# Withdrawing the 64-byte start alignment of the activation and weight part buffers in a two-layer decoder trunk

## The chip, the core and the metric

The kernel runs on one core of a Trainium2 chip. The metric is the device time of one execution in microseconds (us), taken as the median of several runs. The profile is that of one execution. Its span is the time from the first to the last instruction of the core. TensorE is the matrix engine (PE in the profile, its weight loads are PEld), VectorE is DVE, ScalarE is ACT, GpSimd is POOL, and SyncE, which issues most DMAs, is SP.

## What is computed

The reference is a decoder trunk of two layers on 256 positions with 2048 features, in float32. Layer 0 has a recurrent mixer, layer 1 a dilated attention with 16 heads, and each is followed by a squared-ReLU MLP with 8192 hidden features.

```
def squared_relu_mlp(h, w1, w2):
    return jnp.square(jax.nn.relu(h @ w1)) @ w2

def reference(x, ...):
    h = x
    for layer in range(DEPTH):                       # DEPTH = 2
        hn = rms_norm(h, norm_mix[layer])
        if layer % 2 == 0:
            mix = recurrent_mixers(hn, ...)          # w_in, gates, conv, two recurrences, w_out
        else:
            mix = dilated_attention(hn, positions, w_qkv, w_o)
        h = h + mix
        h = h + squared_relu_mlp(rms_norm(h, norm_mlp[layer]), mlp_w1[layer], mlp_w2[layer])
    return rms_norm(h, final_norm)
```

## The kernel before

**Parts.** The matrix products run in TensorE's `float32r` type. To keep float32 accuracy each operand is split into two parts: a rounded one and the remainder. `hi = round(w)` is made by ScalarE (line 104) and `lo = w - hi` by VectorE (line 105). The product of two such numbers is summed from three matmuls, high by high, high by low and low by high. Every matmul goes through the helper `mm`, whose line is 176, so nearly all matmuls of the profile stand under L176.

**Weights.** A weight unit is 128 partitions by 2048 float32, that is 8192 bytes in each partition, fetched by one DMA of SP into one of three `raw` buffers. The class `Weights` (lines 93 to 109) takes one of three `hi` and one of three `lo` buffers for it and splits it. Units are fetched in a fixed order, two ahead of use (`unit`, `fetch`).

**Activations.** `bufa` holds the normalised input of the running layer, `bufb` the output of the mixer or the hidden features of the MLP. Both have for each of 16 blocks of 128 features 256 high and 256 low values, that is 32768 bytes in each partition. `split_to` (lines 228 to 235) writes them.

**Which operand streams.** In `project` (functions `cross` and `direct`) a 128x128 block of `hi` or `lo` is loaded as weights, and `bufa` (in the gates `bufb`) is streamed, 512 or 256 columns at a time. In `tokens` and `products` it is the other way round: a 128x128 block of `bufa`, `bufb` or `forms` is loaded, and 512 columns of `hi` or `lo` are streamed. `forms` holds split sums of activations for a product by seven instead of eight block products in the second matrix of the MLP; it lives in a pool of its own (`pair0`, `pair1`), which exists only during an MLP. A `products` call works in groups of 12 matmuls (four blocks, three part products), each group with `bufb` alone or `forms` alone.

**Order.** The order of the matmuls is written out by hand: every `mm` gets an order dependency on the one before. The other engines are ordered by a planner, from priorities (`stream`, `urgent`) and its own clock. Pools of SBUF tiles are stacked one behind the other in the order of the code: `cst`, `act`, `wraw`, `whi`, `wlo`, `tmp`, and then the pools of each stage, which are closed and reused.

**Where the buffers lie.** This is the memory map of the built kernel before, in bytes from the start of a partition. Every tile's size is rounded up to 32 bytes (the 2056 bytes of `tab_` take 2080). A pool that holds a tile with `align_bytes=64` reserves 32 bytes more for each such tile, and the tile's start is rounded up to 64 within it.

| tile | start | size | start modulo 64 | start modulo 128 |
|---|---|---|---|---|
| first tile of `cst` | 16512 | | 0 | 0 |
| `xall` (first of `act`) | 20800 | 16384 | 0 | 64 |
| `bufa` | 37184 | 32768 | 0 | 64 |
| `bufb` | 70016 | 32768 | 0 | 0 |
| `raw`, first of three | 102784 | 8192 | 0 | 0 |
| `hi`, first of three | 127360 | 8192 | 0 | 0 |
| `lo`, first of three | 152000 | 8192 | 0 | 64 |
| `t1` (first of `tmp`) | 176576 | 1024 | 0 | 64 |
| stage pools, from | 183200 | | 32 | 32 |
| `hz`, first, attention | 195488 | 1024 | 32 | 32 |
| `forms`, layer 0 | 187328 | 16384 | 0 | 64 |
| `forms`, layer 1 | 191424 | 16384 | 0 | 64 |
| `zp`, first, layer 0 | 203712 | 1024 | 0 | 64 |
| `a`, layer 0 | 208832 | 8192 | 0 | 64 |

`bufa` ends at 69952, `bufb` starts 64 bytes later. The last `hi` buffer ends at 151936, the first `lo` buffer starts 64 bytes later. The pool ahead of `forms` in layer 0 ends at 187296, and `forms` starts 32 bytes later; in layer 1 it ends at 191392.

Of the kernel before, what the change touches and what calls it, by code (L numbers as in the profile page):

```python
# [11 lines left out]
F32R = mybir.dt.float32r  # L12
# [7 lines left out]
P = 128  # L20
S = 256
D = 2048
KB = D // P
# [17 lines left out]
def trunk_kernel(ctx, tc, x, xtok, cols, tab, masks, pos, fin, w_in, w_gate, w_out, w_qkv, w_o, w1, w2, out):  # L41
# [3 lines left out]
    act = pool("act")  # L45
    wraw = pool("wraw", 3)
    whi = pool("whi", 3)
    wlo = pool("wlo", 3)
# [9 lines left out]
    xall = act.tile([P, KB * S], F32, name="xall")  # L58
    xin = xall.rearrange("p (k s) -> p k s", s=S)
    xres = xall.rearrange("p (j d) -> p j d", j=2)  # L60
    bufa = act.tile([P, KB, 2 * S], F32R, name="bufa", align_bytes=LINE)
    bufb = act.tile([P, KB, 2 * S], F32R, name="bufb", align_bytes=LINE)

    units = []
    made = {}
# [27 lines left out]
    class Weights:  # L93
        def __init__(self, raw, step=2048):
            self.raw = raw
            self.hi = whi.tile([P, 2048], F32R, name="hi", align_bytes=LINE)
            self.lo = wlo.tile([P, 2048], F32R, name="lo", align_bytes=LINE)
            for at in range(0, 2048, step) if step else ():
                self.split(at, step)

# [754 lines left out]
LINE = 64  # L855
# [108 lines left out]
```

## Time and profile before

| | |
|---|---|
| time, median of 3 runs | 2227.1 us (2226.89 to 2227.21) |
| the profiled execution's own time | 2227.31 us |
| its span | 2225.5 us |
| granted TensorE clock, mean | 0.998 |
| PE busy | 2207.2 us (99%), 12004 matmuls |
| PEld busy | 1892.6 us (85%) |
| DVE busy | 1673.0 us (75%) |
| ACT busy | 1110.0 us (50%) |
| DMA | 431.25 MB, mean 194 GB/s |

The busy times of PE count the overlap of successive matmuls once, and the end of a matmul is modelled; what a stream of matmuls really costs is seen best from where the next one starts, that is from the chain of work that ended last, whose pieces have a start, a length and a count. In the groups of instructions, `p<-hi,bufb` reads: output `p`, inputs `hi` and `bufb`, with the line, the number of instructions after an x, the busy time in all and the mean of one in ns, and then the idle time of the engine ahead of them and what ended it.

### The profile page before, as it was taken

How to read it: one execution, taken by the hardware profiler on the slowest of the kernel's cores; microseconds unless marked ns; L12 is line 12 of the kernel's file. 1: busy time of each engine (PE TensorE's matmuls, PEld its weight loads, DVE VectorE, ACT ScalarE, POOL GpSimd, SP SyncE). 2: the span in 40 equal slices, each digit the busy share in tenths (PEclk: the TensorE clock that was granted, in tenths of full speed). 3: DMA queues.
4: the chain of work that ended last, by engine and by line, in shares of the span. 5: the costliest groups of instructions: out<-in, count | busy, mean ns of one | idle time of the engine just before them, and what ended most of it. 6: DMA issues, size and time to landing. Idle time of an engine off the chain costs nothing.

```text
span 2225.5 us, 29702 instructions
## 1 busy us (share of the span) xinstructions
PE 2207.2 (99%) x12004; PEld 1892.6 (85%) x12004; DVE 1673.0 (75%) x2286; ACT 1110.0 (50%) x1364; POOL 15.8 (1%) x23
## 2 busy tenths in 40 slices
PE   9999999999999999999999999999999999999997
PEld 8999998888888888888888888888878888888886
DVE  8777796578777877877867878556787687687787
ACT  6444585444445444544654444444454454454454
POOL 0000000000000000000000000000000000000000
PEclk9999999999999999999999999999999999999999
DMA  8444446556655755755654544655566567566553
GB/s 312 163 158 163 158 154 228 180 185 203 229 187 186 242 196 174 244 199 159 208 207 158 182 173 164 224 179 185 158 218 241 171 201 247 188 189 246 190 189 114
DMA packets 61017, 431.25 MB, mean 194 GB/s; under 512 B 6784, under 2 KB 7552, under 8 KB 9424
## 3 DMA queue, kind: packets, MB, share of 16 engines
q1 hardware_dynamic: 58320, 412.20, 52.8%
q0 software_dynamic: 2560, 17.16, 4.2%
q8 instruction: 94, 1.54, 0.3%
q14 instruction: 43, 0.35, 0.0%
HBM read 427.48 MB, written 2.10 MB: 193 GB/s over the span
## 4 chain that ended last, share of the span: by engine, by line
PE 95%; DVE 3%; ACT 1%; DMA 0%; issue 0%; SPq 0%; ACTq 0%; DVEq 0%
PE p L176 81%; PE po L176 6%; PE pd L176 5%; DVE lo L105 1%; PE pl L471 1%; ACT hi L104 1%; PE pl L179 0%; DVE a L142 0%; PE pl L777 0%; PE po L798 0%; DMA xall<-in_x 0%; PE pd L790 0%; DMA a<-in_w 0%; DVE bufa L234 0%; PE pd L455 0%
## 5 line engine op out<-in xcount | busy, mean ns | idle before, releaser
L105 DVE TENSOR_TENSOR lo<-raw,hi 128x1024 fp32r<-128x1024 f32 (+2 forms) x486 | 822.1, 1709 | 359.3 <-ACT hi L104 339.2
L104 ACT CAST hi<-raw 128x1024 fp32r<-128x1024 f32 (+2 forms) x486 | 688.3, 1441 | 685.2 <-PE p L176 524.9
L176 PE MATMUL p<-bufa,hi 128*128 128x512 f32 (+1 forms) x3840 | 862.8, 359 | 2.4 <-DVE bufa L234 2.3
L176 PEld LDWEIGHTS p<-bufa,hi 128*128 128x128 f32 x3840 | 668.1, 188 | 104.8 <-DVE bufa L234 3.8
L176 PE MATMUL p<-bufa,lo 128*128 128x256 f32 x3200 | 517.6, 283 | 0.0
L176 PEld LDWEIGHTS p<-bufa,lo 128*128 128x128 f32 x3200 | 449.4, 188 | 14.2
L176 PE MATMUL p<-hi,bufb 128*128 128x512 f32 x1408 | 458.0, 395 | 0.2 <-DVE xall L650 0.2
L176 PEld LDWEIGHTS p<-hi,bufb 128*128 128x128 f32 x1408 | 264.4, 188 | 64.1 <-DVE xall L650 3.1
L176 PE MATMUL p<-lo,bufb 128*128 128x512 f32 x704 | 277.8, 395 | 0.3 <-DVE lo L105 0.2
L104 ACT CAST hi<-a 128x2048 fp32r<-128x2048 f32 x64 | 122.0, 1906 | 160.9 <-PE p L176 83.6
L105 DVE TENSOR_TENSOR lo<-a,hi 128x2048 fp32r<-128x2048 f32 x64 | 146.5, 2289 | 55.5 <-ACT hi L104 55.4
L176 PEld LDWEIGHTS p<-lo,bufb 128*128 128x128 f32 x704 | 132.1, 188 | 33.1 <-DVE lo L105 2.7
L176 PE MATMUL p<-hi,bufa 128*128 128x512 f32 x384 | 125.1, 400 | 0.4 <-ACT hi L104 0.4
L176 PEld LDWEIGHTS p<-hi,bufa 128*128 128x128 f32 x384 | 72.3, 188 | 16.7 <-ACT hi L104 1.3
L176 PE MATMUL pd<-hi,bufb 128*128 128x512 f32 x256 | 85.5, 395 | 0.1
L176 PE MATMUL po<-hi,bufb 128*128 128x512 f32 x256 | 85.4, 394 | 0.1
L176 PE MATMUL p<-hi,forms 128*128 128x512 f32 x256 | 85.4, 394 | 0.0
L176 PE MATMUL p<-lo,bufa 128*128 128x512 f32 x192 | 76.5, 399 | 1.8 <-DVE lo L105 1.8
L142 DVE TENSOR_TENSOR a<-a,raw 128x2048 f32<-128x2048 f32 x32 | 73.0, 2282 | 0.0
L223 ACT COPY t<-p 128x256 f32<-128x256 f32 x128 | 47.0, 367 | 41.4 <-PE p L176 41.1
L650 DVE SCALAR_TENSOR_TENSOR xall<-p,nm,xall 128x512 f32<-128x512 f32 x64 | 47.7, 746 | 24.7 <-PE p L176 24.7
L230 ACT CAST bufb<-zp 128x256 fp32r<-128x256 f32 x128 | 50.8, 404 | 17.2 <-DVE zp L684 17.1
(239 smaller groups left out, 1807.9 us busy)
## 6 DMA issues: line engine op xcount, KB each, us to landing
raw<-in_w SPq DMA_DIRECT2D x224, 1024.0 KB, 4.8
raw<-in_w_qkv SPq DMA_DIRECT2D x48, 1024.0 KB, 4.8
raw<-in_w_in SPq DMA_DIRECT2D x46, 1024.0 KB, 4.8
raw<-in_w_out SPq DMA_DIRECT2D x16, 1024.0 KB, 4.8
a<-in_w SPq DMA_DIRECT2D x16, 1024.0 KB, 4.8
t<-in_w SPq DMA_DIRECT2D x16, 1024.0 KB, 4.9
t<-in_w POOLq DMA_DIRECT2D x16, 1024.0 KB, 8.0
raw<-in_w_o SPq DMA_DIRECT2D x16, 1024.0 KB, 4.9
```

Of the source, the lines that this page charges most:

```text
L104: A.copy(h, w)
L105: V.tensor_tensor(l, w, h.bitcast(F32), OP.subtract)
L142: V.tensor_tensor(r, r, held[add], OP.add)
L176: chain[:] = [after(T.matmul(*args, **kw), chain)]
L223: A.copy(t, p[:, S:])
L230: A.copy(dst[:, :S], src)
L471: T.matmul(pl[:, j], kq[:, js], halves(qp[:, js], c, True), start=True, stop=True)
L650: V.scalar_tensor_tensor(xres[:, j, at], bank, (r2 if sign > 0 else r2n)[:, j:j + 1], xres[:, j, at], op0=OP.mult, op1=OP.add)
```

## The change

The four tiles `bufa`, `bufb`, `hi` and `lo` are asked for without a start alignment. Nothing else of the program is edited: every instruction, its shape, its order dependency and its priority stand as before. `forms`, the buffer of the activation sums, keeps its alignment of 64 bytes in both layers (`LINE = 64`).

```
-    bufa = act.tile([P, KB, 2 * S], F32R, name="bufa", align_bytes=LINE)
-    bufb = act.tile([P, KB, 2 * S], F32R, name="bufb", align_bytes=LINE)
+    bufa = act.tile([P, KB, 2 * S], F32R, name="bufa")
+    bufb = act.tile([P, KB, 2 * S], F32R, name="bufb")
...
     class Weights:
         def __init__(self, raw, step=2048):
             self.raw = raw
-            self.hi = whi.tile([P, 2048], F32R, name="hi", align_bytes=LINE)
-            self.lo = wlo.tile([P, 2048], F32R, name="lo", align_bytes=LINE)
+            self.hi = whi.tile([P, 2048], F32R, name="hi")
+            self.lo = wlo.tile([P, 2048], F32R, name="lo")
```

## The prediction

> **What bounds the kernel now.** I read the page first: span, busy shares and the chain that ended last.
>
> ```profile
> span 2225.5 us, 29702 instructions
> PE 2207.2 (99%) x12004; PEld 1892.6 (85%) x12004; DVE 1673.0 (75%) x2286; ACT 1110.0 (50%) x1364; POOL 15.8 (1%) x23
> PE 95%; DVE 3%; ACT 1%; DMA 0%; issue 0%; SPq 0%; ACTq 0%; DVEq 0%
> PE p L176 81%; PE po L176 6%; PE pd L176 5%; DVE lo L105 1%; PE pl L471 1%; ACT hi L104 1%; PE pl L179 0%; DVE a L142 0%; PE pl L777 0%; PE po L798 0%; DMA xall<-in_x 0%; PE pd L790 0%; DMA a<-in_w 0%; DVE bufa L234 0%; PE pd L455 0%
> ```
>
> The kernel is a stream of matmuls: 92% of the span is L176 on the chain that sets the end. The splitting of the weights (L104, L105) is on it with 2%. So a change of where buffers lie is worth something only through the pace of the L176 matmuls, or if splitting or DMA became so slow that PE waits. Next I read the groups, shapes kept apart, for the pace of each operand pair; these rows carry all that follows.
>
> ```profile
> L176 PEld LDWEIGHTS p<-bufa,hi 128*128 128x128 f32 x3840 | 668.1, 188 | 104.8 <-DVE bufa L234 3.8 <-DVE hz L411 0.3
> L105 DVE TENSOR_TENSOR lo<-raw,hi 128x2048 fp32r<-128x2048 f32 x224 | 512.7, 2290 | 221.8 <-ACT hi L104 218.6 <-ACT bufb L230 3.2
> L176 PE MATMUL p<-hi,bufb 128*128 128x512 f32 x1408 | 458.0, 395 | 0.2 <-DVE xall L650 0.2
> L104 ACT CAST hi<-raw 128x2048 fp32r<-128x2048 f32 x224 | 428.1, 1911 | 463.2 <-PE p L176 377.9 <-PE po L176 54.5 <-PE pd L176 16.1
> L176 PE MATMUL p<-lo,bufb 128*128 128x512 f32 x704 | 277.8, 395 | 0.3 <-DVE lo L105 0.2
> L176 PEld LDWEIGHTS p<-hi,bufb 128*128 128x128 f32 x1408 | 264.4, 188 | 64.1 <-DVE xall L650 3.1
> L105 DVE TENSOR_TENSOR lo<-a,hi 128x2048 fp32r<-128x2048 f32 x64 | 146.5, 2289 | 55.5 <-ACT hi L104 55.4
> L176 PE MATMUL p<-hi,bufa 128*128 128x512 f32 x384 | 125.1, 400 | 0.4 <-ACT hi L104 0.4
> L104 ACT CAST hi<-a 128x2048 fp32r<-128x2048 f32 x64 | 122.0, 1906 | 160.9 <-PE p L176 83.6 <-DVE a L142 47.1 <-PE pd L176 18.9
> L176 PEld LDWEIGHTS p<-hi,bufa 128*128 128x128 f32 x384 | 72.3, 188 | 16.7 <-ACT hi L104 1.3
> L176 PE MATMUL p<-lo,bufa 128*128 128x512 f32 x192 | 76.5, 399 | 1.8 <-DVE lo L105 1.8
> L176 PE MATMUL p<-lo,forms 128*128 128x512 f32 x128 | 51.0, 399 | 0.0
> ```
>
> The reader is to see that a 512-column matmul takes 394 to 400 ns whichever buffer is streamed and loaded, that every weight load takes 188 ns, and that ScalarE and VectorE split a unit in about 1.91 and 2.29 us wherever it comes from.
>
> **The change part by part.** First, what it does to the addresses, since no instruction changes. I worked this out from the sizes in the code and the map of the kernel before. `bufa` starts where it did, at 37184: the tile ahead of it ends on a multiple of 64, so the request never moved it. Without the 32 reserved bytes of each of the two aligned tiles of `act`, `bufb` starts right at the end of `bufa`, 37184 + 32768 = 69952 = 1093 x 64. The `raw` buffers follow at 69952 + 32768 = 102720 = 1605 x 64, `hi` at 102720 + 3 x 8192 = 127296 = 1989 x 64, `lo` at 151872 = 2373 x 64, `tmp` at 176448 = 2757 x 64. So all of them are still multiples of 64: the sizes are, and the stack reaches them at one. Everything from `tmp` on moves down by 128 bytes and keeps its remainder, `forms` too (187200 and 191296, by its own request). What moves in the low bits is this: `bufb`, `raw` and `hi` go from a multiple of 128 to 64 beyond one; `bufa`, `lo`, `forms` stay 64 beyond one.
>
> Then the costs, each by a pair of rows that differs in that bit already. Streaming `hi` (and `lo`, past weights from `bufb`, `forms` or `bufa`, in `products` and `tokens`): before, `hi` starts at a multiple of 128 and `lo` does not, and `p<-hi,bufb` and `p<-lo,bufb` take 395 and 395 ns. Cost 0. Loading `hi` as weights: it becomes what `lo` is; the loads of `bufa` and of `bufb`, one on each side of that bit, take 188 and 188 ns, as the loads of `hi` itself do, and PEld sits idle for 104.8 us ahead of those. Cost 0.
>
> Loading `bufb`: it becomes what `bufa` and `forms` are, and here the means do differ a little, 395 against 400 and 399 ns. Ends of matmuls are modelled, so I looked at starts: first the chain of waits through `w_out` (96 matmuls with `bufb`) and through `products` (12 at a time; in this order with `bufb`, `forms`, `forms`, `bufb`), then the timeline of PE through a value projection of layer 1, which loads `bufa`.
>
> ```profile
> 362.95 22.28 PE p L176 x96
> ...
> 518.44 2.79 PE pd L176 x12
> ...
> 529.79 2.81 PE pd L176 x12
> ...
> 540.97 2.81 PE pd L176 x12
> ...
> 546.56 2.78 PE pd L176 x12
> ```
>
> ```profile
> 1139.19 0.63 PE L176 MATMUL p<-hi,bufa 128*128 128x512 f32 x2
> 1139.66 0.39 PE L176 MATMUL p<-lo,bufa 128*128 128x512 f32 x1
> ...
> 1146.13 0.63 PE L176 MATMUL p<-hi,bufa 128*128 128x512 f32 x2
> ```
>
> With `bufb`, 12 matmuls take 22.28 / 8 = 2.785 us or 2.78 to 2.79. With `bufa`, ten times three matmuls take 1146.13 - 1139.19 = 6.94 us, so 12 take 2.776. With `forms` they take 2.81. The start of `bufa` has the bit and is not slower, so the bit is not what makes `forms` slower; `forms` differs in more, for its high and low parts are 2048 bytes apart and those of `bufb` 1024. I take 0. The end above is that `bufb` comes to the price of `forms`: 2880 matmuls (1408 + 704 in `p`, 384 each in `pd` and `po`, rows below) are 240 groups at 2.81 - 2.785 = 0.025 us, +6.0 us. The end below is that the 768 matmuls with `forms` (16 calls of `products`, four groups of 12 in each), whose distance to `hi` changes by 64 bytes, come to 2.785: 64 groups, -1.6 us.
>
> ```profile
> L176 PE MATMUL pd<-hi,bufb 128*128 128x512 f32 x256 | 85.5, 395 | 0.1
> L176 PE MATMUL po<-hi,bufb 128*128 128x512 f32 x256 | 85.4, 394 | 0.1
> L176 PE MATMUL pd<-lo,bufb 128*128 128x512 f32 x128 | 50.4, 394 | 0.0
> L176 PE MATMUL po<-lo,bufb 128*128 128x512 f32 x128 | 50.4, 394 | 0.0
> ```
>
> Splitting: after the change `raw`, `hi` and `lo` start at the same remainder to 8192, as `raw` and `hi` do before. The tile `a` stands at another one, and `hi<-a` against `hi<-raw` is 1906 to 1911 ns, `lo<-a,hi` against `lo<-raw,hi` 2289 to 2290. No row has `lo` and `raw` at one remainder; at most I allow the 5 ns by which the ScalarE rows differ, 288 times 1.4 us, on two engines with 25% and 50% of idle time. On the path: 0.
>
> DMA into `raw`: it lands 64 bytes beyond a multiple of 128 after the change, which is where `a` lands before.
>
> ```profile
> raw<-in_w SPq DMA_DIRECT2D x224, 1024.0 KB, 4.8
> a<-in_w SPq DMA_DIRECT2D x16, 1024.0 KB, 4.8
> q1 hardware_dynamic: 58320, 412.20, 52.8%
> ```
>
> Both take 4.8 us, and a fetch is two units ahead. The cover, if it were slower, is the other half of the DMA engines' time. Cost 0.
>
> The order of instructions has no term: the planner goes by priorities and by which buffers are free, and tiles that share memory share it as before, since all the stage pools move by the same 128 bytes.
>
> The sum is 0. The profiled execution took 2227.31 us, 1.8 us more than its span, and 0.2 us more than the median of 2227.1; so the forecast is 2227.1 us. About 0.2%, 4.5 us, is what a measurement of this kernel can tell from no change.
>
> One thing I can't see is a `float32r` operand that starts off 64 bytes, because there is none before. The nearest rows are plain float32 matmuls: `hz`, at 32 beyond a multiple of 64, and `tab_` and `xall`, on multiples.
>
> ```profile
> L179 PE MATMUL pl<-tab__179,xall 128*128 128x128 f32 x96 | 12.4, 272 | 0.0
> L776 PE MATMUL pl<-hz 128*128 128x128 f32 x32 | 6.1, 272 | 0.0
> L415 DVE TENSOR_TENSOR hz<-p,t 128x256 f32<-128x256 f32 x32 | 13.2, 411 | 0.0
> L225 DVE TENSOR_TENSOR zp<-p,t 128x256 f32<-128x256 f32 x128 | 53.5, 418 | 4.4 <-ACT t L223 4.4
> ```
>
> They are equal on PE, 272 and 272 ns, and VectorE writes the unaligned `hz` in 411 ns and the aligned `zp` in 418. By these a start off 64 bytes is free; but float32 streams slower for each column than `float32r`, so for the latter I keep an upper end. It is one 64-byte piece more to read for each streamed operand, an estimate: 16 of 512 columns of 22.28 / 96 = 0.232 us is 7.25 ns, times 2880 + 768 + (384 + 192 with `bufa`) = 4224 streams of `hi` and `lo` is +30.6 us. It is paid only if a start falls off 64, which the arithmetic above excludes. The Trainium skill, SBUF — State Buffer, section Specifications (TRN2), gives "16-byte" cachelines as what a read should stay in; by that rule every start at a step of 32 bytes begins on a line, and this end would be 0 and not 30.6 us. The rows of `hz` and `xall` agree as far as float32 shows it; no run here shows it for `float32r`.
>
> **The rivals.** First, slower: loading `bufb` from 64 beyond a multiple of 128 costs what loading `forms` does. For it speak the 399 ns and the 2.81 us of `forms`, against it the 2.776 us of `bufa`, which has the same bit. It would give 2227.1 + 6.0 = 2233.1 us, slower by 0.27%. It decides from 0.019 us a group, 4.5 / 240.
>
> Second, slower: the tiles are not where I put them, and `hi` or `lo` comes to 32 beyond a multiple of 64, and the streams pay for it: 2227.1 + 30.6 = 2257.7 us. For it speaks that `forms` did need its 32 bytes, so starts off 64 exist in this stack; against it that all the tiles ahead of `lo` have sizes that are multiples of 64 and that the map of before fits the rule to the byte in five places. If that happens at half the price it is slower still, from 1.1 ns a stream.
>
> Third, faster: `forms` gets the pace of `bufb` because its distance to `hi` changes. That gives 2227.1 - 1.6 = 2225.5 us, which is within 0.2%. To go past 0.2% the dense stream as a whole would have to quicken; 4.5 us over the 12004 matmuls of the page is 0.4 ns each. Against it: before, `hi` and `lo` stand at different distances to `bufb` in that bit, and are streamed in the same 395 ns.
>
> **How the numbers follow.** No change in the pace: 0.87. First rival 0.05, second 0.02, third 0.04, of which 0.01 past 0.2%; another order or an effect of the addresses that no row shows, of either sign and past 0.2%, 0.02. So faster 0.02, within 0.2% 0.90, slower 0.08. The forecast is 2227.1 us. The range takes in both ends of the cost of loading: from 2225.5 to 2233.1 us.
>
> **What would show it.** Right: the same number of instructions on each engine; `p<-hi,bufb` and `p<-lo,bufb` within 1 ns of 395; groups of 12 with `bufb` at 2.78 to 2.79 us; weight loads at 188 ns; L104 and L105 at 1.91 and 2.29 us; DMA into `raw` at 4.8 us; idle time of PE as before. The first rival would show as groups of `bufb` at 2.81 us with the others unchanged, the second as longer streams of `hi` and `lo` in all of L176, the third as `forms` at 2.785 us. The prediction would be wrong by a cause I have not priced if L104 or L105 grew and PE's waits for them with it, or if the instructions stood in another order.

## The result and the profile after

The changed kernel takes 2206.7 us (median of 4 runs, 2206.14 to 2207.49) against 2227.14 us. The ratio is 0.9909 with a 95% interval of 0.9892 to 0.9926: 0.9% faster. The prediction was 2227.1 us, range 2225.5 to 2233.1: wrong.

Every engine runs the same instructions in the same order, and the memory map is the one worked out in the prediction (`bufb` 69952, `raw` 102720, `hi` 127296, `lo` 151872, `forms` 187200 and 191296). So addresses alone did this. First the page of the kernel after: span, busy times, the chain that ended last.

```profile
span 2204.3 us, 29702 instructions
PE 2180.6 (99%) x12004; PEld 1897.7 (86%) x12004; DVE 1673.1 (76%) x2286; ACT 1110.0 (50%) x1364; POOL 15.8 (1%) x23
PE 84%; DVE 9%; ACT 3%; DMA 2%; issue 1%; SPq 0%; ACTq 0%; DVEq 0%
```

PE is busy for 26.6 us less with the same 12004 matmuls. It is idle for 2204.3 - 2180.6 = 23.7 us, before 2225.5 - 2207.2 = 18.3, so 5.4 us of the gain went into waits. VectorE's share of the chain grew from 3% to 9%; that is the work through which the chain runs at those waits, not their length. Its busy time did not change. The groups, shapes kept apart, answer to those of the prediction:

```profile
L176 PE MATMUL p<-bufa,hi 128*128 128x512 f32 x2560 | 615.1, 392 | 2.4 <-DVE bufa L234 2.4
L176 PE MATMUL p<-bufa,lo 128*128 128x256 f32 x3200 | 521.9, 285 | 0.0
L105 DVE TENSOR_TENSOR lo<-raw,hi 128x2048 fp32r<-128x2048 f32 x224 | 512.7, 2290 | 209.5 <-ACT hi L104 206.3 <-ACT bufb L230 3.1
L176 PE MATMUL p<-hi,bufb 128*128 128x512 f32 x1408 | 451.9, 391 | 1.6 <-DVE xall L650 1.6
L104 ACT CAST hi<-raw 128x2048 fp32r<-128x2048 f32 x224 | 428.1, 1911 | 446.6 <-PE p L176 367.6 <-PE po L176 52.0 <-PE pd L176 13.0
L176 PE MATMUL p<-lo,bufb 128*128 128x512 f32 x704 | 275.3, 391 | 3.8 <-DVE lo L105 3.8
L176 PE MATMUL p<-hi,bufa 128*128 128x512 f32 x384 | 123.6, 396 | 0.7 <-ACT hi L104 0.7
L176 PE MATMUL p<-lo,forms 128*128 128x512 f32 x128 | 49.8, 389 | 0.0
```

Splitting is untouched (2290 and 1911 ns as before). All matmuls with 512 columns are shorter, 391 for 395 with `bufb` and, where `lo` is streamed past `forms`, 389 for 399. The row of 256 columns, `p<-bufa,lo`, takes 285 ns, 2 more than before. Here are the rows of before for the streams of `bufa`, which the prediction did not show, and from its chain the first product of an MLP quarter (16 units, 256 matmuls of 512 columns and 256 of 256):

```profile
L176 PE MATMUL p<-bufa,hi 128*128 128x512 f32 x2560 | 625.9, 396 | 2.3 <-DVE bufa L234 2.3
L176 PE MATMUL p<-bufa,lo 128*128 128x256 f32 x3200 | 517.6, 283 | 0.0
...
602.58 89.85 PE p L176 x512
```

The same place in the chain of the kernel after, with a matrix of `w_out` (96 matmuls with `bufb`) and groups of 12 in `products` (in this order with `forms`, `bufb`, `bufb`):

```profile
364.12 21.81 PE p L176 x96
...
581.23 2.72 PE po L176 x12
583.95 2.72 PE p L176 x12
586.67 2.72 PE po L176 x12
...
600.27 89.02 PE p L176 x512
```

The 96 take 21.81 us instead of 22.28, and groups of `forms` and of `bufb` cost the same now, 2.72 us instead of 2.81 and 2.78.

For the rest of this text the pace is worked out from the start times in the trace: the mean time from the start of one matmul to that of the next of its kind, leaving out those over 0.52 ns a column, which are waits. Which passages between groups are counted moves a mean by up to 0.2 ns. Before, the starts of a `products` group never settle (in a typical one 236, 237, 226, 235, 239, 234 ns with `forms`); after, they lie between 225 and 228. After the change a stream of `bufa` past `hi` needs some five matmuls of a unit to reach 227 ns, which makes its mean 228.4; before, it goes on alternating between 231 and 236. The gain by kinds of matmul:

| kind | count | before, ns | after, ns | us |
|---|---|---|---|---|
| `bufa` past `hi`, 512 columns | 2560 | 232.9 | 228.4 | -11.5 |
| `bufa` past `lo`, 256 columns, in `cross` | 2560 | 118.7 | 119.5 | +2.0 |
| `bufa` past both, 256 columns, in `direct` | 1920 | 118.2 | 119.7 | +2.9 |
| `hi`, `lo` past `bufb` | 2880 | 232.0 | 227.0 | -14.4 |
| `hi`, `lo` past `forms` | 768 | 234.0 | 226.7 | -5.6 |
| `hi`, `lo` past `bufa` | 576 | 231.6 | 228.4 | -1.8 |

That is -28.4 us; with 5.4 us more of idle PE it is -23.0, against -21.2 of the spans. Counted from start to start with every gap left in, the `L176` matmuls of 256 and 512 columns take 2124.1 us for 2145.0, which is 20.9 us less. So nearly all of the gain lies in them, and the waits and the passages from one kind to the next took back 7.5 us, more than the modelled ends of the matmuls show as idle time.

### The profile page after: what moved, and what is told of

The parts are those of the page before. It is cut to its first block, busy times and chain, and to the rows that moved or that the text cites. A ratio compares the mean times of both kernels' runs of the same rounds, so it can differ in the third digit from the quotient of the medians.

```text
span 2204.3 us, 29702 instructions
## 1 busy us (share of the span) xinstructions
PE 2180.6 (99%) x12004; PEld 1897.7 (86%) x12004; DVE 1673.1 (76%) x2286; ACT 1110.0 (50%) x1364; POOL 15.8 (1%) x23
## 3 DMA queue, kind: packets, MB, share of 16 engines
q0 software_dynamic: 2560, 17.16, 4.3%
## 4 chain that ended last, share of the span: by engine, by line
PE 84%; DVE 9%; ACT 3%; DMA 2%; issue 1%; SPq 0%; ACTq 0%; DVEq 0%
PE p L176 75%; DVE lo L105 5%; PE po L176 5%; DVE a L142 2%; ACT hi L104 2%; DMA a<-in_w 2%; PE pd L176 1%; PE pl L471 1%; DVE xall L650 1%; PE pl L179 0%; PE pl L777 0%; DVE bufa L234 0%; PE po L798 0%; DMA xall<-in_x 0%; PE pd L790 0%
## 5 line engine op out<-in xcount | busy, mean ns | idle before, releaser
L176 PE MATMUL p<-bufa,hi 128*128 128x512 f32 (+1 forms) x3840 | 854.5, 357 | 2.4 <-DVE bufa L234 2.4
L176 PEld LDWEIGHTS p<-bufa,hi 128*128 128x128 f32 x3840 | 672.0, 190 | 95.2 <-DVE bufa L234 3.8
L176 PE MATMUL p<-bufa,lo 128*128 128x256 f32 x3200 | 521.9, 285 | 0.0
L176 PEld LDWEIGHTS p<-bufa,lo 128*128 128x128 f32 x3200 | 452.6, 191 | 12.7
L176 PE MATMUL p<-hi,bufb 128*128 128x512 f32 x1408 | 451.9, 391 | 1.6 <-DVE xall L650 1.6
L176 PEld LDWEIGHTS p<-hi,bufb 128*128 128x128 f32 x1408 | 264.5, 188 | 59.1 <-DVE xall L650 5.0
L176 PE MATMUL p<-lo,bufb 128*128 128x512 f32 x704 | 275.3, 391 | 3.8 <-DVE lo L105 3.8
L176 PEld LDWEIGHTS p<-lo,bufb 128*128 128x128 f32 x704 | 132.3, 188 | 33.7 <-DVE lo L105 7.2
L176 PE MATMUL p<-hi,bufa 128*128 128x512 f32 x384 | 123.6, 396 | 0.7 <-ACT hi L104 0.7
L176 PEld LDWEIGHTS p<-hi,bufa 128*128 128x128 f32 x384 | 72.3, 188 | 16.0 <-ACT hi L104 1.6
L176 PE MATMUL pd<-hi,bufb 128*128 128x512 f32 x256 | 84.3, 390 | 0.2 <-DVE xall L650 0.2
L176 PE MATMUL po<-hi,bufb 128*128 128x512 f32 x256 | 84.2, 390 | 0.3 <-DVE xall L650 0.3
L176 PE MATMUL p<-hi,forms 128*128 128x512 f32 x256 | 84.1, 389 | 0.0
L176 PE MATMUL p<-lo,bufa 128*128 128x512 f32 x192 | 76.3, 397 | 1.8 <-DVE lo L105 1.8
```

The source lines that it names most:

```text
L176: chain[:] = [after(T.matmul(*args, **kw), chain)]
```

## The experiments

**The theories.** After the change `bufa`, `bufb`, `hi`, `lo` and `forms` all start at 64 modulo 256; before, they start at 64, 128, 128, 192 and 192. Theory D (distance): the pace of PE depends on how the start of the streamed buffer stands to that of the buffer whose blocks are loaded as weights. Theory S (place): a start 64 beyond a multiple of 128 is fast by itself. Theory W: reads of PE are disturbed by ScalarE and VectorE unless `raw`, `hi` and `lo` stand at one remainder. Blocks inside the buffers are multiples of 512 bytes apart, so the starts stand for all.

The buffers are moved by unused tiles between the pools; no instruction is added. For room in e2, e3 and e4, three small tiles of the last lines share the buffers of others, and `bufb` has a pool of its own, so that it can stand elsewhere in the stack.

```
     gap = lambda n, b: pool("gap_" + n).tile([P, b // 4], F32, name="gap_" + n)
...
     # e1: all together            gap("front", 64); act = pool("act")
     # e2: lo alone                gap("lo", 64); wlo = pool("wlo", 3); tmp = pool("tmp", 2); gap("stages", 128)
     # e3: hi alone, behind lo     gap("hi", 64); whi = pool("whi", 3)
     # e4: bufb alone, behind lo   gap("bufb", 64); actb = pool("actb")
```

Of the sixteen runs only e11, e12 and e13 were timed several times; each of the others is one execution.

**e1, all buffers 64 bytes further.**

> A gap of 64 bytes ahead of the buffers moves bufa, bufb, raw, hi, lo and forms together: their distances are those of the kernel after, but all of them now start at a multiple of 128. Theory D (distance: PE slows when the streamed buffer and the buffer loaded next stand at different remainders to 128 or 256): as the kernel after, 2206.7 us within 0.1%, starts of 512-column matmuls 227 ns apart in the steady stream. Theory S (place: a start 64 beyond a multiple of 128 is the fast one): as the kernel before or slower, 2227 us, 231 to 235 ns.

**e2, `lo` alone 64 bytes further.**

> From the kernel after, lo alone moves up by 64 bytes; hi, bufa, bufb and forms keep their places. Theory D: groups of 12 with bufb or forms, where lo is streamed between two streams of hi, lose their steady 227 ns and go back to about 231 to 235; the 512-column stream of bufa past hi keeps 227; the 256-column stream of bufa past lo goes from 119.5 back to about 118.7 ns. In all between 2210 and 2225 us. Theory S: lo at a multiple of 128 slows where lo is read only. Theory W (ScalarE and VectorE, reading raw and hi and writing lo, disturb PE's reads unless raw, hi and lo stand at one remainder): everything slows at once, the stream of bufa past hi too, 2227 us.

**e3, `hi` alone.**

> From the kernel after, hi alone moves by 64 bytes (its buffers now lie behind those of lo, so its upper address changes too). Theory D: the stream of bufa past hi goes back to about 233 ns for 512 columns, groups of 12 back to 231 to 235; about 2220 to 2230 us, the larger part of the 20 us lost. Theory S: the same sign, as hi is at a multiple of 128. Theory W: everything slows, 2227 us.

**e4, `bufb` alone.**

> From the kernel after, bufb alone moves by 64 bytes (it now lies behind lo). Theory D: groups of 12 with bufb slow to 231 to 235 ns a matmul, those with forms and the streams of bufa past hi and lo keep 227 and 119.5; 2880 matmuls by 5 ns less what VectorE's waits hide, 2212 to 2222 us. Theory S: the same place slows. Theory W: nothing slows, 2206.7 us, since raw, hi and lo keep their distances.

Measured: 2206.36, 2213.84, 2230.78 and 2219.71 us. From the chains, in the order e1, e2, e3, e4, a matrix of `w_out` (weights from `bufb`, streams of `hi` and `lo`) and a first product of the MLP (streams of `bufa`):

```profile
364.29 21.80 PE p L176 x96
...
600.50 89.02 PE p L176 x512
```

```profile
362.62 22.26 PE p L176 x96
...
600.93 88.64 PE p L176 x512
```

```profile
362.63 22.40 PE p L176 x96
...
602.82 90.05 PE p L176 x512
```

```profile
365.03 22.41 PE p L176 x96
...
604.08 89.05 PE p L176 x512
```

e1 keeps both lengths of the kernel after, although all starts are at multiples of 128 now: theory S falls. e4 leaves `raw`, `hi` and `lo` at one remainder and still slows the matmuls with `bufb` (233.3 ns), while the streams of `bufa` stay at 228.5 and those past `forms` at 228.0: theory W falls. e3, where `hi` is off all three of its partners, slows all kinds of 512 columns, to 233 ns, and ends 3.5 us above the kernel before. e2 shows what the prediction could not see: `hi` past `bufb` is at distance 0 there, and yet it runs at 232 ns, because in its groups of three `lo` at another distance stands between two streams of `hi`. One pair off its place takes the steady pace from the whole group. e2 also shows that 256-column streams like a distance: `bufa` past `lo` runs at 117.5 ns, and the first product of the MLP gets shorter, 88.64 for 89.02 us.

**Alignment itself, and the period.** The next four runs ask whether a start off 64 bytes costs anything, and at which distances PE is fast again. In three of them each kind of pair has a distance of its own, so that one run measures three.

```
     # e5: all, 32 bytes           gap("front", 32); ... ; gap("stages", 32); forms without align_bytes
     # e6: hi, lo +32, bufb +128, forms +160 against the kernel after
     # e7: bufb +96, hi, lo +128, forms 0
     # e8: bufb +128, hi, lo +256, forms +32
```

> A gap of 32 bytes ahead, and forms without its own request: all six buffers keep the distances of the kernel after, but every one starts 32 beyond a multiple of 64, which is what the alignment excluded. If only distances count: 2206.5 us within 0.1%, 227 ns. If a start off 64 bytes costs one more piece for each streamed operand, as my second rival had it: 4224 streams of 512 and 4576 of 256 columns by up to 7 ns, up to 2260 us.

> Measures three distances (streamed start minus loaded start) at once: bufa past hi and lo -32, hi and lo past bufb -96, hi and lo past forms -128. Theory D with a period of 128 bytes: forms runs at 227 ns, bufa and bufb wobble at 231 to 235. With a period of 256 or more: all three wobble. If what counts is a common line of 64 bytes, -32 would be half as bad as -64: about 230 ns. The 256-column streams past lo leave 119.5 for 117.5 to 118.7 where their distance is not 0. About 2222 to 2232 us if bufa and bufb are slow.

> Three more: bufa past hi and lo -128, hi and lo past bufb +32, hi and lo past forms +128. With a period of 128 bytes bufa runs at 227 and 119.5 ns and forms at 227, bufb at 231 to 235: about 2215 to 2220 us. With a period of 256 all wobble: 2225 to 2232 us.

> Tests the period from above: bufa past hi and lo -256, hi and lo past bufb -128, hi and lo past forms -32. With a period of 256 (or 128) bytes bufa runs at 227 and 119.5 ns; with a period of 512 it wobbles, 231 to 235. bufb as in the two runs ahead of it at 128, forms slow as at 32. 2212 to 2232 us.

Measured: 2206.24, 2233.03, 2231.79 and 2220.42 us. The same two rows of the chains of e5, e6, e7 and e8:

```profile
364.26 21.83 PE p L176 x96
...
600.62 89.02 PE p L176 x512
```

```profile
363.83 22.49 PE p L176 x96
...
604.38 89.92 PE p L176 x512
```

```profile
365.05 22.40 PE p L176 x96
...
605.01 89.87 PE p L176 x512
```

```profile
365.03 22.32 PE p L176 x96
...
603.99 89.03 PE p L176 x512
```

e5: starts 32 bytes beyond a multiple of 64 cost nothing, 2206.24 us with the lengths of the kernel after. The 64-byte alignment of these buffers was worth nothing as such. The Trainium skill, SBUF — State Buffer, section Specifications (TRN2), with its 16-byte lines agrees with this. e8 has `bufa` 256 bytes off `hi` and `lo` modulo 512 and is as fast there as at 0 (89.03 us), while 128 (e7 `bufa`, e8 `bufb`), 96 (e6 `bufb`) and 32 (e6 `bufa`, e7 `bufb`, e8 `forms`) are slow, 232 to 234 ns. So, on steps of 32 bytes, the period is 256 bytes, and nothing speaks for half the harm at 32: `bufa` past `hi` runs at 233.2 ns there.

**The change by halves.** From the kernel before, the alignment is withdrawn from two of the four tiles.

```
     # e9:  bufa and bufb without align_bytes; hi and lo as before
     # e10: hi and lo without align_bytes; bufa and bufb as before
```

> Half of the change: the alignment is withdrawn from bufa and bufb alone. By the map this puts bufa, bufb and hi at one remainder to 256 and lo and forms 64 beyond it. Theory D: bufa past hi keeps 227 to 228.5 ns, bufa past lo falls to about 117.5; every group of 12 matmuls in products and tokens has a stream at a distance (lo past bufb and bufa, hi past forms) and goes at 231 to 233. The same pattern as with lo alone moved, so 2213 to 2216 us. If the gain of the change belonged to single buffers and not to pairs, half of it or so would be here: 2217 us and no slow groups.

> The other half: the alignment is withdrawn from hi and lo alone. By the map bufb, hi, lo and forms come to one remainder to 256 and bufa 64 below it. Theory D: products and w_out, w_o at 227 ns; bufa past hi at 233 (2560 by 4.6 ns = +11.8 us against the kernel after), hi and lo past bufa at 232 (576 by 4 = +2.3), bufa past lo and the direct streams of 256 columns at about 117.6 (4480 by 1.9 = -8.5): 2206.7 + 5.6 = 2212 us.

e9 takes 2213.72 us, as expected: all groups with `hi` and `lo` streamed at 232 to 234 ns, `bufa` past `lo` at 117.6. e10 takes 2195.43 us, where 2212 was expected: faster than the whole change by 11 us. I timed it again, with an interval, and then varied the distance of `bufa` alone, with `hi`, `lo`, `bufb` and `forms` at one remainder.

> The kernel with the alignment withdrawn from hi and lo alone, timed with an interval. If one look was right: 2195 to 2196 us, ratio to the kernel before 0.985 to 0.988, 256-column streams past hi and lo at 113.8 ns again.

```
     # e14, e16: bufa in a pool of its own behind wlo, gap("bufa", 64) and gap("bufa", 32)
     # e15:      gap("bufb", 96) ahead of bufb, raw, hi, lo; forms along with them
```

> All at one remainder except bufa, which lies 64 bytes above (in the half change it lay 64 below). If only the size of the distance counts for the 256-column streams: 113.8 ns and 2195 us. If the sign counts: between 114 and 119.5 ns, 2195 to 2212 us. 512-column streams of bufa near 233 in both.

> All at one remainder except bufa, which lies 96 bytes below. If 113.8 ns at -64 is the bottom of a broad valley between 118.6 (-32) and 119.0 (-128): 114 to 117 ns, 2195 to 2206 us. If it is a single place: about 118.5 ns and 2214 to 2218 us.

> All at one remainder except bufa, which lies 32 bytes above. -32 gave 118.6 ns and 233.2. If the sign does not count the same: 2215 to 2220 us with products at 227. If it counts, anything between 113 and 119.5 ns.

Measured: e13 2196.07 us (4 runs, 2195.42 to 2196.34), ratio to the kernel before 0.9859, interval 0.9843 to 0.9875; e14 2199.03, e15 2216.81, e16 2209.93 us. First the groups of e13 that differ from the kernel after, then the two chain rows of e13, e14, e15 and e16:

```profile
L176 PE MATMUL p<-bufa,hi 128*128 128x512 f32 x2560 | 627.0, 396 | 2.4 <-DVE bufa L234 2.4
L176 PE MATMUL p<-bufa,lo 128*128 128x256 f32 x3200 | 503.5, 278 | 0.0
L176 PE MATMUL p<-bufa,hi 128*128 128x256 f32 x1280 | 229.1, 280 | 0.1
```

```profile
355.37 21.79 PE p L176 x96
...
591.39 88.76 PE p L176 x512
```

```profile
361.84 21.81 PE p L176 x96
...
597.29 88.27 PE p L176 x512
```

```profile
361.73 21.80 PE p L176 x96
...
599.20 90.22 PE p L176 x512
```

```profile
360.25 21.81 PE p L176 x96
...
597.12 89.56 PE p L176 x512
```

All four keep the fast 96 matmuls of `w_out`, 21.79 to 21.81 us. What differs is the stream of `bufa`, by the distance of `bufa` to both `hi` and `lo` (pace in ns):

| distance of `bufa`, bytes | 512 columns past `hi` | 256 columns, `cross` | 256 columns, `direct` | run |
|---|---|---|---|---|
| 0 | 228.4 | 119.5 | 119.7 | after |
| +32 | 233.3 | 116.8 | 117.0 | e16 |
| +64 | 229.3 | 115.8 | 117.6 | e14 |
| 128 | 232.8 | 118.7 | 119.2 | e7 |
| -96 | 234.1 | 118.4 | 117.9 | e15 |
| -64 | 232.9 | 113.8 | 113.8 | e13 |
| -32 | 233.2 | 118.6 | 118.2 | e6 |

So the sign counts, there is no valley, and the two widths want different distances. Against the kernel after, e13 loses 2560 x 4.5 ns = 11.5 us on the 512-column streams and 0.6 on `tokens` with `bufa`, and gains 2560 x 5.7 = 14.6 and 1920 x 5.9 = 11.3 us on those of 256 columns: -13.8 us, against -10.6 measured; from start to start with every gap left in, these matmuls take 2113.4 us for 2124.1, which is -10.7. My 2212 us failed mainly on one number: I took 117.6 ns from e2 and e3, where only one of `hi` and `lo` was 64 off, and with both at -64 it is 113.8. e13 is the fastest version of this study.

The distance alone does not explain that number. In `cross` the matmuls past `lo` run in stretches of 16 with no other pair among them, and in e2, e9 and e13 `bufa` is 64 below `lo` in the same way. Yet from the fifth matmul on, every full stretch goes at 117.9 ns in e2 and e9 and at 113.3 in e13. In e14 both paces occur in one run: of its 145 full stretches 71 go at 113.3 ns and 74 at 117.8, mostly in turn, so its 115.8 in the table is a mean of two. Two neighbouring stretches of e14 of 16 matmuls, from the timeline:

```profile
628.35 2.05 PE L176 MATMUL p<-bufa,lo 128*128 128x256 f32 x16
...
633.91 1.98 PE L176 MATMUL p<-bufa,lo 128*128 128x256 f32 x16
```

So one distance allows two steady paces with 256 columns. What leads a stretch into the one or the other is not shown. The 512-column stream of `bufa` at +64, where e14 was expected near 233 ns, takes 229.3, and the pairs with the roles changed bear the sign out: `hi` and `lo` past `bufa` take 229.4 ns in e13, where they lie 64 above it, and 233.3 in e14, where they lie 64 below.

**The waits that took 5 us back.** Here the weight loads' waits, before and after:

```profile
PEld p L176 <- DVE lo L105: 6.2, 13, 1.1
PEld p L176 <- DVE xall L650: 3.1, 8, 0.6
```

```profile
PEld p L176 <- DVE lo L105: 10.7, 14, 1.1
PEld p L176 <- DVE xall L650: 5.0, 8, 0.9
```

To see whether VectorE's load in `products` is the cause, the addition for `t4` was given to a DMA, on the kernel after and on the kernel before.

```
+        if T3_DMA and what == "d":
+            nc.gpsimd.dma_start(held["a"], src[i], accum_op=OP.add)
-        if T3_DMA and what == "t3":
+        if T3_DMA and what in ("t3", "t4"):
             add = None
```

> On the kernel after: the sum a + d of the products t4 is made by a DMA that adds while it writes, as that of t3 already is, so VectorE has 16 additions of 2.28 us less in the products stages and 16 DMAs of 1 MB more run on GpSimd's queue. If VectorE is what keeps part of the gain back there (PE idle 23.7 us against 18.3 before), PE's idle time falls by up to those 5.4 us: 2200 to 2205 us. Rival: the DMA engines or the later arrival of a + d cost as much or more: 2206 to 2212 us.

> The same edit on the kernel before. If VectorE became late only through the faster stream, the relief is worth less here than on the kernel after: 2224 to 2227 us. If VectorE held PE back before as well, it is worth as much in both.

Measured: 2206.07 us (ratio to the kernel before 0.9905, 0.9889 to 0.9922) and 2226.77 us (0.9999, 0.9989 to 1.0008). The page of e11, and the wait in it:

```profile
span 2204.0 us, 29748 instructions
PE 2180.6 (99%) x12004; PEld 1896.5 (86%) x12004; DVE 1638.8 (74%) x2270; ACT 1110.3 (50%) x1364; POOL 29.6 (1%) x39
```

```profile
PEld p L178 <- DVE lo L105: 11.1, 15, 1.3
```

VectorE has 34.3 us less to do, and PE's idle time stays (2204.0 - 2180.6 = 23.4 us). So the load of VectorE over the stage is not what PE waits for, unless the later arrival of the sum cost as much, which these runs do not separate. The chain of the kernel after shows where the waits stand, where an MLP quarter goes from its first product to `products`:

```profile
689.29 2.20 DVE a L142
691.49 2.20 DVE lo L105
693.69 0.33 DVE zp L225
694.03 0.66 DVE xall L650
694.69 2.20 DVE lo L105
```

VectorE has an addition and two splits in a row there, while PE comes out of the first product earlier than before; the addition that e11 took away comes later. The same pieces stand on the chain of the kernel before, from 692.43 us on, so the queue itself is not new. That it is the cause fits both runs, but a run that empties it was not made, so it is argued and not shown.

## Why the prediction was wrong, point by point

- **The addresses**: right to the byte. So were the unchanged instructions, the splitting at 2290 and 1911 ns, the DMAs and the loads, 188 ns with `bufb`. Loads of `hi` beside streams of `bufa` came to 190 ns instead of 188.
- **The step that failed** is "the costs, each by a pair of rows that differs in that bit already". It took the low bits of one buffer at a time, modulo 128, and compared 395 with 395 and 2.785 with 2.776 us. What counts is a relation of two buffers, modulo 256, and, where pairs alternate in a group, of all of them. Before, only two pairs stood at distance 0, `hi` past `bufb` and `lo` past `forms`, and each in a group with another pair off it; so every row of before was a slow one, and equal rows meant equally slow, not free. e2 and e9 show it: `hi` past `bufb` at distance 0 runs at 232 ns beside a `lo` that is off, and at 227 in the kernel after.
- **The terms mis-sized by it.** Loading `bufb`, taken as 0, was worth -14.4 us. Loading `hi` as weights, also 0, was worth -11.5 us in the 512-column streams of `bufa` past it, and the 256-column streams past `hi` and `lo` lost 4.9 us; the prediction judged this term by the length of the loads and the idle time of PEld and did not ask for the pace of the stream that runs meanwhile. The end below, -1.6 us for `forms`, had the right sign and named the distance to `hi`, but its floor was the slow pace of `bufb`, 2.785 us for 12; both came to 2.72, and `forms` gained 5.6 us.
- **The first rival**, that `bufb` would come to the price of `forms`: wrong; both got the lower price. **The second**: excluded by the addresses, and e5 shows that its price was 0 and not 30.6 us, as the rows of `hz` and `xall` had said. **The third**, a dense stream that quickens as a whole, is what happened with 512 columns, but not with 256, where it slowed; I dismissed it because `hi` and `lo` went at 395 ns at different distances to `bufb`, the same misreading.
- **A sign in the rows of before that I passed over**: groups of 12 that take 2.78 and 2.81 us, and starts that wobble between 224 and 241 ns among equal matmuls. I read the mean of a stream that does not settle as a floor. The sign holds for the streams of 512 columns here; with 256 columns the unsettled stream of before (115 to 123 ns in a stretch past `lo`, mean 118.2 once it runs) is faster than the settled one after, at 120.0.

## What to carry to other kernels

When TensorE is the bound and works on `float32r` operands as here, with a weight load for every matmul, look at the times from start to start of equal matmuls. If those of 512 columns don't settle, try the starts of the streamed and of the loaded buffers at one remainder to 256 bytes, all pairs of a group together. Then try a few distances for streams of 256 columns, where a settled pace can still be the slow one. What an alignment request buys can be an accident of where it puts the next buffer; padding by 32 or 64 bytes tells, without touching an instruction. A row that equals another row is not a floor unless a case is known that differs in what is changed.

## What was not expected of the hardware

The pace of `float32r` matmuls depends on the distance of the streamed to the loaded buffer: with 512 columns 227 ns at a distance of 0 modulo 256 bytes, 229 to 234 at the others tried; with 256 columns 119.5 at 0 and, at -64, 113.8 in e13 but 117.5 in e2, so there the distance is not all that counts. The Trainium skill, TensorE: Matmul & The Clock Gate, Part 2, says that loading the next weights takes no read bandwidth from the running matmul, the two having ports of their own; here the place of the weights changes the pace of the stream, and the measurement decides. What in the hardware makes it so stays open: the traces show only the pace, and not whether it is the reads that collide.
